# Short four-band TensorE products: the loop over the bands moves inside the loop over terms

## The chip, the core and the metric

The kernel runs on one core of a Trainium2 chip. The metric is the device time of one execution in microseconds (us); the kernel before takes 1805.59 us, the median of three runs (1805.42 to 1806.01). TensorE is called PE here, VectorE DVE, ScalarE ACT, GpSimd POOL and SyncE SP.

## What is computed

Two layers work on 128 context and 256 latent tokens of 1024 features. Each layer is a half-step SwiGLU, a mixing sub-layer and another half-step SwiGLU, each behind a norm that is modulated by a conditioning vector. The modulation is a product of that vector with a matrix of 1024 x 9216 per layer:

```python
mod = (jax.nn.silu(cond) @ P['w_mod'][l] + P['b_mod'][l]).reshape(cond.shape[0], N_MOD, 1, D_MODEL)
...
z = h @ P['w_in'][l]
z_a, z_b, z_c = jnp.split(z, [S5_WIDTH, S5_WIDTH + 2 * CONV_WIDTH], axis=-1)
y_a, h_final = _s5_branch(z_a, P, l, h0)
```

One branch of the mixer is a complex-diagonal state-space scan (S5) with 32 groups of 16 channels and 64 states per direction. The kernel runs the scan in chunks of eight tokens, and for that it computes tables on the chip from the S5 parameters: a matrix from a chunk's inputs to the state, one from the state to the outputs, and the kernel inside a chunk, which is the product of the first factor of one (`bp`, `bb`) with the other (`my`, `cT`, `nci`).

## The kernel before

PE's instructions run in the order in which the program is written; the other engines have an order of their own, laid down when the program is built. Almost all of PE's work is the large projections: each weight unit (512 KB) is fetched by SP's queue into `wr`, split by ACT (`wh`, line 126) and DVE (`wl`, line 105) into a high and a low part, and multiplied in three passes (lines 198 to 200), 24 products of 384 columns for a full unit. Three buffers hold the splits, so a new split can begin only when PE has left the unit three before it. After each unit the projection calls `tick()`, which lets side work go one step on: modulation (`mod_group`, line 385, and `mod_wide`, line 427), the S5 tables (`s5_tables`), and the mixer's own side steps.

`s5_tables(l)` goes through 32 groups, four at a time: eight **blocks** per layer, sixteen in all. In a block DVE first makes `my` and `mt` over several ticks. Then PE writes one PSUM bank in four bands of 32 partitions, one band for each group `s`: two terms `i` of `bp` with `my` over 128 columns (line 1013), then two terms over 16 columns from `bb` with `cT` and `nci` (line 1022). ACT copies the bank to `kall` (line 1030). PE then turns eight 128 x 128 tiles of `mt` (line 138): four into the other bank of the two in `ps_tb`, four into the first bank again, for which they need the copy to `kall` to be over. ACT copies both (`ms`, line 1038). POOL's queue sends `my`, `ms` and `kall` to memory.

`mod_wide` sums weighted rows on DVE into two accumulators and ends with a similar product (line 427): four bands, two terms `i`, 256 columns. It runs four times. `mod_group` (line 385) has four bands too, but there the loop over the bands `s` is already the innermost, inside the loop over `k`.

Both operands of these products are f32, and the profile shows such a product as two records; a line that is run 128 times has 256 records.

Of the kernel before, what the change touches and what calls it, by code (L numbers as in the profile page):

```python
# [16 lines left out]
PSUM = bass.MemoryType.PSUM  # L17
# [18 lines left out]
H = 16  # L36
# [20 lines left out]
def hybrid_step(ctx: ExitStack, tc: tile.TileContext, I, pos_r, pos_c, y_prompt, y_sample, new_state):  # L57
# [70 lines left out]

# [1 line left out]
    ident = cst.tile([P, P], F32, tag="ident", name="ident")  # L130
# [8 lines left out]

# [1 line left out]
    early = {"on": True}  # L141
# [62 lines left out]

    # short products, spread among the long ones
    small = deque()
# [34 lines left out]
    def proj(srcs, xs, nt=NT, kfirst=False, between=None):  # L241
        """PSUM tiles [feature tile, tokens] of xs @ src for each [K, 256] source in turn, alternating along K."""
        n = srcs[0].shape[0] // P
        out = [(mm_bank(), mm_bank()) for _ in srcs]
        for k0, k1 in kparts(n):
            for s, o in zip(srcs, out):
                u = next_unit(s[k0 * P : k1 * P, :])
                if kfirst:
                    order = [(k, m) for k in range(k0, k1) for m in range(2)]
                else:  # L250
                    order = [(k, m) for m in range(2) for k in range(k0, k1)]
                for k, m in order:
                    mm3(o[m][:, :nt], u, xs[k], k - k0, mcols(m), k == 0, k == n - 1)
                    if between and m:
                        between()
                tick()
        return out if len(srcs) > 1 else out[0]

# [1 line left out]
    x = [cst.tile([P, NT], F32, tag=f"x{k}", name=f"x{k}") for k in range(KD)]  # L260
# [30 lines left out]

# [1 line left out]
    pv_t = []  # L293
# [38 lines left out]

# [1 line left out]
    silu_c = cst.tile([P, KD, 32], F32, tag="silu_c", name="silu_c")  # L334
# [18 lines left out]
    def mod_group(l, q):  # L353
        """q: 2048 columns from 2048 q on, or (0, half): that half of the tiles of the first shift and scale"""
        half = isinstance(q, tuple)
# [55 lines left out]
    def mod_wide(l, c0, n=WU):  # L411
        """n columns from c0 on, summed over the 128-row tiles ahead of the tensor engine's sum over the rows"""
        acc = [c4([P, WU], f"macc{s}") for s in range(2)]
        for k in range(KD):
            raw = m6([P, WU], "modw")
            nc.sync.dma_start(raw, I["w_mod"][l][k * P : (k + 1) * P, c0 : c0 + WU])
            for s in range(2):
                if k == 0:
                    act.activation(acc[s], raw, AF.Copy, scale=silu_c[:, k, s : s + 1])
                else:  # L420
                    stt(acc[s], raw, silu_c[:, k, s : s + 1], acc[s])
                yield
        w = WU // 4
        b = ax_bank()
        for s in range(4):
            for i in range(2):
                pe.matmul(
                    b[32 * s : 32 * s + 32, :w],
                    pick[:, i, :],
                    acc[i][:, s * w : (s + 1) * w],  # L430
                    start=(i == 0),
                    stop=(i == 1),
                    skip_group_check=True,
                )
        yield
        mod_out(l, b, [c0 + s * w for s in range(4)], w)
        yield
# [23 lines left out]

# [1 line left out]
    class Stats:  # L463
# [17 lines left out]
        def preload(self, t):  # L481
            """the square root's table, ahead of its use"""
            act.activation(self.std[:, 3:4], t[:, 0:1], AF.Sqrt, bias=eps_t)
            self.loaded = True
# [15 lines left out]
    def bcast_diag(dg):  # L500
        """[128 tokens, 3] on diagonals -> every partition holds all 384 values (in PSUM)."""
        b = ax_bank()
# [3 lines left out]
    class Lead:  # L506
        """The norm in front of a sub-layer.

        The first products take x times the norm's and the modulation's scales, with the shifts as two more
        columns, and the root mean square divides their results; by then the normed tokens are there for the rest.  # L510
        """

# [53 lines left out]
        def result(self, b):  # L566
            """(product over the root mean square, what the shifts add to it) of a first product's bank"""
            t = tmp("ld")
# [6 lines left out]
    class First:  # L575
        """The norm of the tokens as they come in: the modulation arrives last, in halves of the features."""

# [47 lines left out]

# [1 line left out]
    def ffn_srcs(l, j):  # L627
# [71 lines left out]

# [1 line left out]
    ms_d = [drm.tile([P, G, 2, P], F32, tag=f"ms{l}", name=f"ms{l}") for l in range(DEPTH)]  # L701
# [42 lines left out]
    def exp_(out, a, w):  # L744
        """out <- exp(a): 2^k times the series of the remainder; w: four scratch planes"""
        xx, kk, rr, pp = (w[:, i] for i in range(4))
# [29 lines left out]
    def s5_params(raw, ldt):  # L776
# [20 lines left out]
        yield  # L797
        # sine and cosine of a_im dt: reduced to [-pi, pi], then the half angle's series
        mul(th, aim, dtb)
# [32 lines left out]
        br, bi = pw[:, 0, 1], pw[:, 1, 1]  # L832
        # q = (abar - 1) / a
        mul(den, are, are)
# [12 lines left out]
        yield  # L847
        # powers of abar
        done = 1
        while done < TC:  # L850
# [5 lines left out]
            yield  # L856
        # powers as the chunk matrices need them: [to state, from state]
        lo_i = slice(TC - 1, None, -1), slice(1, TC + 1)
# [10 lines left out]
        yield  # L869
        # unit rotation per chunk  # L870
        cur = e1
# [40 lines left out]
    def s5_tables(l):  # L912
# [25 lines left out]
        for gb in range(G // GB):  # L938
# [24 lines left out]
            for sb in range(GB // GS):  # L963
# [44 lines left out]
                b = tb_bank()  # L1008
                for s in range(4):
                    g = s0 + s  # L1010
                    rows = slice(32 * s, 32 * s + 32)
                    for i in range(2):
                        pe.matmul(  # L1013
                            b[rows, : TC * H],
                            bp[:, i, g, :],
                            my[:, s, i].rearrange("p i h -> p (i h)"),
# [3 lines left out]
                        )  # L1020
                    for i in range(2):
                        pe.matmul(  # L1022
                            b[rows, TC * H : 9 * H],
                            bb[:, i, g, :],
                            cT[:, 0, g, :] if i == 0 else nci[:, g, :],
                            start=(i == 0),
# [26 lines left out]

# [1 line left out]
    def gelu_sig(t, src):  # L1055
        """t <- sigmoid of the tanh form's argument, so that gelu(src) = src * t"""
        act.activation(t, src, AF.Square, scale=math.sqrt(GELU_A))
# [30 lines left out]
    def mixer(l, ld, nxt):  # L1088
# [6 lines left out]

        # incoming states of the latent sequence
        srow = s1([P, 2, PS, 2], "srow")[:G]
        gq.dma_start(srow, I["state_ssm"][0, l].rearrange("d g p r -> g d p r"))
        h0 = s1([P, 2, G], "h0")

        # S5 input
        zd = drm.tile([G, H, TC, NCH], F32, tag=f"z_d{l}", name="z_d")
# [158 lines left out]
        def activate(t):  # L1261
# [3 lines left out]
            y2 = tmp("y2")  # L1265
            ci = lambda v: v.rearrange("p (c i) -> p c i", i=TC)  # noqa: E731
            stt(ci(y2), zp[:, t].rearrange("p (j c) -> p c j", j=TC), pv[:, 48 + t : 49 + t], ci(b[:, :NT]))
# [19 lines left out]

        # spatial gating
        sg = {}
# [17 lines left out]
        def sg_bias():  # L1307
            # ln_b[c] * sum_k w[q, k] + b[q], for the folded affine of the norm
            b = tb_bank()
# [82 lines left out]

        # conv branch
        pads = []
# [66 lines left out]
        def side():  # L1461
            f = lambda fn, *a: (fn, a)  # noqa: E731
            tap = [f(conv_taps, j, min(j + 3, CONV_K)) for j in range(0, CONV_K, 3)]
# [47 lines left out]

        # spatial gating: first half, feature major
        bu = ld.proj(cols(w_in, 1024))
        for m in range(2):
# [3 lines left out]
            us.append(t)  # L1518
        # spatial gating: second half, token major
        b3 = [mm_bank(), mm_bank(), ax_bank()]  # L1520
# [15 lines left out]

        # conv input
        bb2 = proj([cols(w_in, 768)], hs)
# [14 lines left out]

        # branches, gated
        def gate(br, n):
# [77 lines left out]

# [1 line left out]
    def mod_all(l, qs, after):  # L1635
# [32 lines left out]
    class Final:  # L1668
        """The last norm: tokens times its scale, turned token major; the root mean square divides at the end."""

# [128 lines left out]
def _positions():  # L1799
    """Separable grid embedding, feature major: row part [128, 4, rows], column part [128, 4, width]."""  # L1800
    import numpy as np
# [39 lines left out]
```

## Time and profile before

| | us |
|---|---|
| median of the runs | 1805.59 |
| profiled execution, from first to last instruction | 1802.9 |
| PE busy | 1778.9 |
| ACT waiting for line 1022 (16 times) | 21.2 |

The runs count 2.7 us that lie around the span. A record of PE has a start and a modelled end; successive products overlap in their tails, so durations must not be added up: the distance from one start to the next is what a record costs. "PE" are products, "PEld" the loads of the stationary operand in front of each.

### The profile page before, as it was taken

To read this page: it belongs to the slowest core of one execution; us is meant where nothing else is said; L and a number is where in the kernel's file an instruction comes from. 1 tells how busy PE (TensorE), PEld (TensorE's weight loads), DVE (VectorE), ACT (ScalarE), POOL (GpSimd) and SP (SyncE) were. 2 spreads that over 40 slices of the span, in tenths; PEclk is the share of its full clock that TensorE was granted. 3 is DMA by queue.
4 is the path that set the end of the run, shared out by engine and by line. 5 is a ranking of instruction groups with operands and counts; after the bars stand their busy time and mean duration, and the time that the engine had idled before them with its cause. 6 is when DMAs were issued, how large, how long until landed. Compare 5 with 4: busy or idle time off the path is not lost.

```text
span 1802.9 us, 29079 instructions
## 1 busy us (share of the span) xinstructions
PE 1778.9 (99%) x11186; PEld 1695.1 (94%) x11186; DVE 1248.1 (69%) x2344; ACT 796.0 (44%) x1330; POOL 202.8 (11%) x400
## 2 busy tenths in 40 slices
PE   7999999999999999999999999999999999999997
PEld 4898999999999989999999899999999999999997
DVE  5495676678996786679386665766799787544445
ACT  4354333475455553233366233245834546423233
POOL 2012343310010000000001133232100000000000
PEclk9999999999999999999999999999999999999999
DMA  9768677666743566778346766557666433434332
GB/s 343 249 217 288 210 237 259 213 197 175 250 144 123 173 229 219 254 271 257 117 129 205 243 203 204 179 187 218 172 198 185 138 124 116 135 123 128 129 123 77
DMA packets 253746, 344.37 MB, mean 191 GB/s; under 512 B 22399, under 2 KB 216651, under 8 KB 253608
## 3 DMA queue, kind: packets, MB, share of 16 engines
q1 hardware_dynamic: 228504, 299.18, 51.7%
q0 software_dynamic: 17088, 39.51, 7.3%
q10 hardware_dynamic: 8016, 3.82, 0.8%
q8 instruction: 88, 1.44, 0.3%
q14 instruction: 50, 0.41, 0.1%
HBM read 309.75 MB, written 32.70 MB: 190 GB/s over the span
## 4 chain that ended last, share of the span: by engine, by line
PE 94%; DVE 2%; DMA 2%; ACT 1%; issue 1%; SPq 0%; DVEq 0%; ACTq 0%
PE mm L198 28%; PE mm L199 28%; PE mm L200 27%; PE ax L385 3%; PE tb L1013 1%; PE tb L1159 1%; PE tb L138 1%; PE tb L1237 1%; DMA modw<-in_w_mod_dram 1%; DMA wr<-in_w_in_dram 1%; DVE wl L105 0%; DVE macc L123 0%; PE ax L503 0%; PE tb L1022 0%; PE ax L138 0%
## 5 line engine op out<-in xcount | busy, mean ns | idle before, releaser
L105 DVE TENSOR_TENSOR wl<-wr,wh 128x1024 fp32r<-128x1024 f32 (+2 forms) x389 | 457.1, 1175 | 367.9 <-ACT wh L126 363.2
L126 ACT ACTIVATE wh<-wr 128x1024 fp32r<-128x1024 f32 (+1 forms) x387 | 395.7, 1023 | 650.2 <-PE mm L199 467.4
L198 PE MATMUL mm<-hh,wh 128*128 128x384 f32 x1840 | 628.1, 341 | 3.1 <-ACT hh L609 3.1
L199 PE MATMUL mm<-hl,wh 128*128 128x384 f32 x1840 | 616.4, 335 | 0.7 <-DVE hl L105 0.7
L200 PE MATMUL mm<-hh,wl 128*128 128x384 f32 x1840 | 616.3, 335 | 0.0
L198 PEld LDWEIGHTS mm<-hh,wh 128*128 128x128 f32 x1840 | 346.0, 188 | 32.6 <-issue 20.1
L199 PEld LDWEIGHTS mm<-hl,wh 128*128 128x128 f32 x1840 | 346.2, 188 | 1.6 <-DVE hl L105 1.2
L200 PEld LDWEIGHTS mm<-hh,wl 128*128 128x128 f32 x1840 | 345.9, 188 | 0.1
L198 PE MATMUL mm<-ah,wh 128*128 128x384 f32 x800 | 271.7, 340 | 0.0
L199 PE MATMUL mm<-al,wh 128*128 128x384 f32 x800 | 269.7, 337 | 0.6 <-DVE al L105 0.6
L200 PE MATMUL mm<-ah,wl 128*128 128x384 f32 x800 | 269.3, 337 | 0.0
L198 PEld LDWEIGHTS mm<-ah,wh 128*128 128x128 f32 x800 | 150.2, 188 | 9.6 <-issue 6.7
L199 PEld LDWEIGHTS mm<-al,wh 128*128 128x128 f32 x800 | 150.2, 188 | 0.9 <-DVE al L105 0.9
L200 PEld LDWEIGHTS mm<-ah,wl 128*128 128x128 f32 x800 | 150.2, 188 | 0.0
L123 DVE SCALAR_TENSOR_TENSOR x<-mm,gt,x 128x128 f32<-128x128 f32 x224 | 83.1, 410 | 33.6 <-PE mm L200 33.1
L198 PE MATMUL mm<-xh,wh 128*128 128x386 f32 x240 | 84.6, 353 | 0.0
L199 PE MATMUL mm<-xl,wh 128*128 128x386 f32 x240 | 82.1, 342 | 0.0
L200 PE MATMUL mm<-xh,wl 128*128 128x386 f32 x240 | 82.0, 342 | 0.0
L126 ACT ACTIVATE ah<-av 128x384 fp32r<-128x384 f32 x82 | 42.1, 518 | 87.0 <-DVE av L105 86.7
L123 DVE SCALAR_TENSOR_TENSOR macc<-modw,silu_c,macc 128x1024 f32<-128x1024 f32 x56 | 69.9, 1277 | 11.0 <-DMA modw<-in_w_mod_dram 10.9
L123 DVE SCALAR_TENSOR_TENSOR cacc<-pad,pv,cacc 128x399 f32<-128x399 f32 x120 | 68.5, 627 | 0.0
L385 PE MATMUL ax<-modw,silu_c 128*32 128x512 f32 (+1 forms) x576 | 63.0, 513 | 0.0
(316 smaller groups left out, 1941.0 us busy)
## 6 DMA issues: line engine op xcount, KB each, us to landing
wr<-in_ffn_w_dram SPq DMA_DIRECT2D x256, 512.0 KB, 3.5
modw<-in_w_mod_dram SPq DMA_DIRECT2D x144, 512.0 KB, 5.0
wr<-in_w_gate_dram SPq DMA_DIRECT2D x48, 512.0 KB, 4.6
wr<-in_w_in_dram SPq DMA_DIRECT2D x24, 512.0 KB, 3.8
my<-my POOLq DMA_DIRECT2D x16, 512.0 KB, 5.1
ms<-ms POOLq DMA_DIRECT2D x16, 512.0 KB, 4.0
m_ms<-ms SPq DMA_DIRECT2D x16, 512.0 KB, 6.7
m_my<-my SPq DMA_DIRECT2D x16, 512.0 KB, 9.9
```

The lines of the kernel that those rows point to most:

```text
L105: (eng or dve).tensor_tensor(out, a, b, op=op)
L123: dve.scalar_tensor_tensor(out, a, s, b, op0=op0, op1=op1)
L126: act.activation(hi, full, AF.Copy)
L138: pe.transpose(out, in_, ident[:rows, :rows])
L198: pe.matmul(out, wh[:, k, cols], xh, start=first, stop=False)
L199: pe.matmul(out, wh[:, k, cols], xl, start=False, stop=False)
L200: pe.matmul(out, wl[:, k, cols], xh, start=False, stop=last)
L385: pe.matmul(b[32 * s : 32 * s + 32, :w], silu_c[:, k, :], raws[i][:, c : c + w], start=(k == 0), stop=(k == KD - 1), skip_group_check=True,)
L1013: pe.matmul(b[rows, : TC * H], bp[:, i, g, :], my[:, s, i].rearrange("p i h -> p (i h)"), start=(i == 0), stop=(i == 1), skip_group_check= ...
L1159: pe.matmul(b[:, g * NCH : (g + 1) * NCH], d["ms"][g // GS][:, g % GS, i, :], U[:, q * GB + g, :], start=True, stop=True,)
L1237: pe.matmul(b[64 * half : 64 * half + NCH, g * P : (g + 1) * P], u, w, start=(n == 0), stop=(n == 2), skip_group_check=True,)
```

## The change

In both places the loop over the bands goes inside the loop over the terms. Before, a band got all its products before the next band got its first; after, each term goes to all four bands before the next term. In the tables the 16-column products, which stood at the end of each band, now stand behind all the 128-column ones. The products, their operands, the bank and the order of the terms inside a band are the same, and nothing is added or removed on any engine. (Comments go too, which moves line numbers.)

```diff
@@ mod_wide
-        for s in range(4):
-            for i in range(2):
+        for i in range(2):
+            for s in range(4):
                 pe.matmul(
                     b[32 * s : 32 * s + 32, :w],
                     pick[:, i, :],
@@ s5_tables
-                for s in range(4):
-                    g = s0 + s
-                    rows = slice(32 * s, 32 * s + 32)
-                    for i in range(2):
+                for i in range(2):
+                    for s in range(4):
                         pe.matmul(
-                            b[rows, : TC * H],
-                            bp[:, i, g, :],
+                            b[32 * s : 32 * s + 32, : TC * H],
+                            bp[:, i, s0 + s, :],
                             my[:, s, i].rearrange("p i h -> p (i h)"),
                             start=(i == 0),
                             stop=(i == 1),
                             skip_group_check=True,
                         )
-                    for i in range(2):
+                for i in range(2):
+                    for s in range(4):
                         pe.matmul(
-                            b[rows, TC * H : 9 * H],
-                            bb[:, i, g, :],
-                            cT[:, 0, g, :] if i == 0 else nci[:, g, :],
+                            b[32 * s : 32 * s + 32, TC * H : 9 * H],
+                            bb[:, i, s0 + s, :],
+                            cT[:, 0, s0 + s, :] if i == 0 else nci[:, s0 + s, :],
                             start=(i == 0),
                             stop=(i == 1),
                             skip_group_check=True,
                         )
```

## Rows read from the trace of the kernel before

**Rows 1.** The page: busy time of the engines; the chain by engine

```profile
PE 1778.9 (99%) x11186; PEld 1695.1 (94%) x11186; DVE 1248.1 (69%) x2344; ACT 796.0 (44%) x1330; POOL 202.8 (11%) x400
...
PE 94%; DVE 2%; DMA 2%; ACT 1%; issue 1%; SPq 0%; DVEq 0%; ACTq 0%
```

**Rows 2.** Windows of the two stretches with blocks: busy us, granted clock, DMA share, GB/s

```profile
170.00:350.00 180.00, 180.00 (x1239) 165.24 (x1239) 122.35 (x207) 65.04 (x107) 61.23 (x116) 1.00 0.73 231
1020.00:1235.00 215.00, 215.00 (x1452) 202.96 (x1451) 138.41 (x235) 75.67 (x118) 63.74 (x120) 1.00 0.61 193
```

**Rows 3.** Waits: engine, tile, line, releaser: us in total, times, longest

```profile
ACT wh L126 <- PE mm L199: 467.4, 221, 5.8
DVE wl L105 <- ACT wh L126: 363.2, 211, 6.0
...
ACT kall L1030 <- PE tb L1022: 21.2, 16, 2.0
...
PEld mm L198 <- ACT wh L126: 7.1, 9, 0.8
```

**Rows 4.** Groups of instructions by line and shape, PE: count, busy us, mean ns

```profile
L1013 PE MATMUL tb<-my,bp 128*32 128x128 f32 x256 | 32.3, 278 | 0.0
...
L427 PE MATMUL ax<-macc,pick 128*32 128x256 f32 x64 | 4.3, 384 | 0.0
```

**Rows 5.** Timeline of PE through one block: start us, us, line, records

```profile
178.68 0.33 PE L199 MATMUL mm<-hl,wh 128*128 128x384 f32 x1
178.86 0.34 PE L200 MATMUL mm<-hh,wl 128*128 128x384 f32 x1
179.12 0.62 PE L1013 MATMUL tb<-my,bp 128*32 128x128 f32 x4
179.59 0.18 PE L1022 MATMUL tb<-cT,bb 128*32 128x16 f32 x1
179.59 0.30 PE L1013 MATMUL tb<-my,bp 128*32 128x128 f32 x1
...
179.65 0.21 PE L1022 MATMUL tb<-nci,bb 128*32 128x16 f32 x2
...
180.53 0.30 PE L1013 MATMUL tb<-my,bp 128*32 128x128 f32 x1
...
180.66 0.49 PE L1013 MATMUL tb<-my,bp 128*32 128x128 f32 x3
180.99 0.21 PE L1022 MATMUL tb<-cT,bb 128*32 128x16 f32 x2
...
181.19 1.11 PE L138 MATMUL tb<-ident,mt 128*128 128x128 f32 x8
182.05 0.42 PE L198 MATMUL mm<-hh,wh 128*128 128x384 f32 x1
```

**Rows 6.** Timeline of PE: a modulation product, bands innermost, 16 records

```profile
19.42 1.07 PE L385 MATMUL ax<-modw,silu_c 128*32 128x256 f32 x16
```

**Rows 7.** Timeline of PE: one end of `mod_wide`, bands outermost, 16 records

```profile
720.67 1.08 PE L427 MATMUL ax<-macc,pick 128*32 128x256 f32 x16
```

**Rows 8.** Timeline of PE, from 720.66 to 720.715 alone: records begun by then

```profile
720.67 0.44 PE L427 MATMUL ax<-macc,pick 128*32 128x256 f32 x4
```

**Rows 9.** Timeline of ACT beside two blocks, the second behind a modulation product

```profile
179.10 1.06 ACT L126 ACTIVATE wh<-wr 128x1024 fp32r<-128x1024 f32 x1 [3.95 <-issue]
181.30 0.29 ACT L1030 ACTIVATE kall<-tb 128x144 f32<-128x144 f32 x1 [1.14 <-PE tb L1022]
...
226.33 1.06 ACT L126 ACTIVATE wh<-wr 128x1024 fp32r<-128x1024 f32 x1 [0.81 <-PE mm L199]
227.29 0.51 ACT L126 ACTIVATE ah<-av 128x384 fp32r<-128x384 f32 x1
229.38 0.29 ACT L1030 ACTIVATE kall<-tb 128x144 f32<-128x144 f32 x1 [1.58 <-PE tb L1022]
```

**Rows 10.** Timeline of DVE ahead of the block of group 5: the last `mt`

```profile
175.95 0.68 DVE L105 TENSOR_TENSOR mt<-tp,tp 128x512 f32<-128x512 f32 x1
```

## The prediction

> **What bounds the kernel now.** I read the page's busy times and its chain of waits first, then windows of the stretches in which the changed lines run, then the waits, and last the records of one block on PE with ACT beside it. The reader is to see that PE has work in 99% of the span and holds 94% of the chain [rows 1], and that in the two stretches with blocks it is busy for all of 180 and all of 215 us, at a granted clock of 1.00 (2.4 GHz), while DVE is at 68 and 64%, ACT at 36 and 35% and the DMA engines at 73 and 61% [rows 2]. The other engines are paced by PE: ACT's splits of the weights wait 467.4 us for PE to leave a buffer, and DVE's wait 363.2 us for ACT's, while PE waits 7.1 us in the whole run for a high part, and no wait for a low part is among the long ones [rows 3]. So a microsecond less of PE's own work in these stretches is a microsecond off the end, as long as the splits keep their lead.
>
> Now one block [rows 5]. The first band's record starts at 179.12, the turning of `mt` at 181.19: 2.07 us for 32 records. Inside a band a 128-column record follows the last after 0.11 us (three take 0.49, of which the last 0.27) and a 16-column one after 0.03 (0.21 less 0.18). The bands stand one behind the other: the second starts at 179.59, the last at 180.53, so a band's turn is 0.94 / 2 = 0.47 us. Only at the seams do two bands run at once: at 179.59 the second band's first record starts in the same hundredth as the first band's fifth, and its last three run beside it, still 0.03 us apart.
>
> That overlap is the key. In a modulation product with the bands innermost, 16 records of 256 columns take 1.07 us in all [rows 6]; at 0.38 us for one [rows 4] this leaves (1.07 - 0.38) / 3 = 0.23 us for each of the three further turns of all four bands. The four bands run at the same time. With the bands outermost `mod_wide` takes 1.08 us for the same 16 records [rows 7], and there four of them have begun within 0.05 us [rows 8]: with four records in a band, PE gets to the other bands by itself. With eight in a band it did not, until three were left [rows 5]. Both places fit a PE that can set aside about three records of a band while it looks for work of another.
>
> **The ends of the modulation sums.** Four blocks of 16 records go from the form of rows 7 to that of rows 6: 4 x 0.01 us, nothing. Were it to lose, the nearest bound is the 0.05 us in which the bands start, so 4 x 0.05 = 0.2 us either way.
>
> **The table products.** There are sixteen blocks (256 records of line 1013, 16 in each) [rows 4], alike but for what stands ahead of them. With all four bands at once a block lasts as long as one band by itself plus the lag between bands. One band, from its first record to the turning of `mt`, is the last band of rows 5: 181.19 - 180.53 = 0.66 us. The lag: four starts within 0.05 us [rows 8], and a row of 16 records with bands innermost is not longer than three turns and one record [rows 6]; I take 0.02. That makes 0.68 us and saves 2.07 - 0.68 = 1.39 us per block, 16 x 1.39 = **22.2 us**. The bound on the worse side: if the 16-column records shared one stream at 0.03 us each, 12 more would stand in line, 0.36 us a block, 5.8 us in all. At the seam of rows 5 they kept their 0.03 us beside another band's record, so I take nothing for it. The better side has no more than the lag, 0.3 us.
>
> **What is late next: ACT.** The copy to `kall` waits for PE in all sixteen blocks now, 21.2 us [rows 3]. With PE done 1.39 us earlier, ACT is not always free. In twelve blocks, those directly behind a weight unit, ACT takes up a split just as the block starts: at 179.10, for 1.06 us, so until 1.04 us into the block [rows 9]. The next operation of ACT may start 0.10 us ahead of a split's recorded end (227.29 against 226.33 + 1.06) [rows 9]. So the copy starts at about 0.94 and ends, 0.29 later, at 1.23 us. The fifth turn needs its bank. Today the copy ends 181.30 + 0.29 - 181.19 = 0.40 us behind the first turn, and the eight turns take 182.05 - 181.19 = 0.86 us [rows 5], their own pace of 0.11 each. So the copy may end until 0.68 + 0.40 = 1.08 without cost, and PE will wait 0.15 us: 12 x 0.15 = **1.8 us** given back. In the other four blocks a modulation product goes ahead; in one of them ACT is done with its splits at 227.29 + 0.51 = 227.80, and the copy, at 229.38 today, would come at 227.99 [rows 9], so nothing is lost. Bounds: 0, if ACT gets free sooner, and if all sixteen paid 0.3 us (a small operation of ACT in between), 4.8.
>
> **Everything else.** No instruction, DMA or semaphore is added. POOL's DMAs of `kall` and `ms` and SP's weight loads keep their order and start earlier with PE. The products' inputs are early: the last `mt` of the first block is done at 176.63, 2.5 us ahead of it [rows 10]; the least of the sixteen. A block that is 1.3 us shorter takes as much from the lead of the next splits; that the splits wait for PE, by 467.4 / 221 = 2.1 us on the average [rows 3], covers it. If that cover were gone in some ticks, each would give back at most its 1.3 us.
>
> **Sum.** 22.2 - 1.8 + 0.0 = 20.4 us off a span of 1802.9: 1782.5. The median stands 2.7 us above the span, so the runs should read 1805.6 - 20.4 = **1785.2 us**.
>
> **A rule that speaks against it.** In rows 6 to 8 all four bands hold the same stationary operand; in the table each group has its own `bp`. The Trainium skill, "TensorE: Matmul & The Clock Gate", Part 3, says that a load of weights overlaps running products only where the row groups differ, and all bands here use all 128 rows. By that rule each load would wait for the products before it, the bands would still follow one another, and the time would stay. The trace does not bear it out: at 179.59 to 179.65 two bands with different operands run together, loads included [rows 5].
>
> **The rivals.**
> 1. *Bands with different operands do not run together beyond the seam.* Then 32 records stay in line, 1805.6, or PE reorders as it does now and the change says nothing. For it: no row shows four different operands at once. Against it: the seam. Chance 0.05.
> 2. *The 16-column part stays in line*: + 5.8 us, and with the copy then ready at 1.15 us the 1.8 us of waiting vanish: 1785.2 + 5.8 - 1.8 = 1789.2. For it: these records are so short that their loads may set the pace. Against it: the 0.03 us kept at the seam. Chance 0.07.
> 3. *Slower: a change of band costs what entering the four-band form costs.* The first record of a block comes 179.12 - 178.86 = 0.26 us after the last projection product, where the one before it came after 0.18: 0.08 us more [rows 5]. A block now changes band 4 times, after it 16. If each change cost that and kept bands apart, 12 x 0.08 = 0.96 us a block, and 4 x 0.08 in each of four sums: 1805.6 + 15.4 + 1.3 = 1822.3. It decides only if changes both cost over 1.39 / 12 = 0.12 us or forbid the overlap. Against it: rows 6, where the band changes at every product and the time is that of rows 7. Chance 0.03.
>
> **How the numbers follow.** The forecast has a chance of 0.85; its own range is 22.5 to 17.4 us off (copy's wait 0 to 4.8), 1783.1 to 1788.2. To hold eight in ten I reach to rival 2 and leave 1.6 us below for waits elsewhere that may fall otherwise: 1781.5 to 1790. A measurement of this kernel can tell about 0.2% (3.6 us) from no change. Faster by more: 0.85 + 0.07 = 0.92; within: 0.05; slower: 0.03.
>
> **What would show it.** In the profile after, a block's line 1013 records should form four quick groups of four, some 0.11 us apart, and the turning of `mt` begin 0.7 us behind the first; at 0.93 rival 2 holds, at 2.07 rival 1. Twelve copies to `kall` should start close behind a split of ACT and no longer wait for line 1022, whose wait falls from 21.2 to about 3 us. The turns should take 0.95 to 1.0 us in these twelve blocks and 0.86 in four. Line 427 should keep its 1.08 us. The prediction is wrong if PE is no longer busy throughout the two stretches, that is, if a split or a DMA comes too late.

## The result: some 20 us less, nearly all of it in sixteen blocks

| | before | after |
|---|---|---|
| median of the runs, us | 1805.8 (four runs, 1805.42 to 1808.8) | 1784.95 (1782.06 to 1785.44) |
| time over time before, 95% interval | 1 | 0.9877 (0.9864 to 0.989) |
| span of the profiled execution, us | 1802.9 | 1783.6 |
| PE busy, us | 1778.9 | 1758.1 |

The kernel is faster, by 1.2%; the forecast was 1785.2. The first block after, on PE (start us, us, engine, line, records), beside [rows 5]:

```profile
181.08 0.34 PE L200 MATMUL mm<-hh,wl 128*128 128x384 f32 x1
181.35 0.65 PE L1012 MATMUL tb<-my,bp 128*32 128x128 f32 x16
181.81 0.23 PE L1022 MATMUL tb<-cT,bb 128*32 128x16 f32 x8
181.87 0.23 PE L1022 MATMUL tb<-nci,bb 128*32 128x16 f32 x8
182.03 1.24 PE L138 MATMUL tb<-ident,mt 128*128 128x128 f32 x8
183.03 0.42 PE L198 MATMUL mm<-hh,wh 128*128 128x384 f32 x1
```

The reader is to see that line 1012 (line 1013 before) is now one row of 16 records, which last 0.65 us together with a tail of 0.27, that the eight and eight short records follow in steps of 0.03 us, each step with all four bands, and that the turning of `mt` begins 182.03 - 181.35 = 0.68 us after the first record, where it took 2.07. The view cut to the first 0.06 us of the block shows four records begun, the last of them 0.02 us behind the first (0.32 less 0.30):

```profile
181.35 0.32 PE L1012 MATMUL tb<-my,bp 128*32 128x128 f32 x4
```

The stretches with blocks are still all PE (busy us of PE, PEld, DVE, ACT, POOL, then granted clock, DMA share, GB/s), as in [rows 2]:

```profile
170.00:350.00 180.00, 180.00 (x1299) 164.59 (x1298) 129.75 (x223) 69.49 (x115) 66.59 (x126) 1.00 0.78 247
1010.00:1220.00 210.00, 210.00 (x1482) 197.11 (x1481) 141.76 (x244) 77.49 (x123) 67.66 (x127) 1.00 0.66 204
```

PE has 1299 records in the 180 us that held 1239, at the same granted clock, and the DMA engines go from 73 to 78% in the first stretch: the work is packed tighter and nothing else has become the bound. The waits that answer to [rows 3]:

```profile
ACT wh L126 <- PE mm L199: 483.9, 227, 5.8
DVE wl L105 <- ACT wh L126: 350.2, 202, 4.8
...
PEld mm L198 <- ACT wh L126: 7.1, 9, 0.8
```

```profile
ACT kall L1030 <- PE tb L1022: 2.0, 4, 0.7
```

PE waits as little for a split as before, and ACT's wait for line 1022 has fallen from 21.2 us in sixteen places to 2.0 in four.

**Where the time went.** From the first record of a block to the product behind its turns (a projection's, in two blocks a modulation's) PE spends, summed over the sixteen blocks and read from the starts of their rows, 47.1 us before and 26.6 after: 20.5 less. The span loses only 19.3, because this profiled execution happened to get to its first projection product 2.05 us later than the one before (25.47 against 23.42 us from the start). Past that point the two traces keep step unit by unit, but for the sixteen blocks and 0.8 us at one stall behind 824 us that is gone. Elsewhere the time outside the blocks did not change.

### The profile page after: what moved, and what is told of

The parts are those of the page before. It is cut to its first block, busy times and chain, and to the rows that moved or that the text cites. A ratio compares the mean times of both kernels' runs of the same rounds, so it can differ in the third digit from the quotient of the medians.

```text
span 1783.6 us, 29079 instructions
## 1 busy us (share of the span) xinstructions
PE 1758.1 (99%) x11186; PEld 1672.6 (94%) x11186; DVE 1247.1 (70%) x2344; ACT 795.0 (45%) x1330; POOL 202.8 (11%) x400
## 4 chain that ended last, share of the span: by engine, by line
PE 97%; DVE 1%; DMA 1%; ACT 1%; issue 0%; DVEq 0%; ACTq 0%
PE mm L198 30%; PE mm L199 29%; PE mm L200 29%; PE ax L385 3%; PE tb L1159 1%; PE tb L138 1%; PE tb L1237 1%; DMA wr<-in_w_in_dram 1%; PE tb L1012 0%; PE ax L503 0%; PE ax L138 0%; DMA crow<-in_c_dram 0%; DVE sqacc L105 0%; PE mm L1528 0%; PE ax L489 0%; PE mm L1530 0%
## 5 line engine op out<-in xcount | busy, mean ns | idle before, releaser
L123 DVE SCALAR_TENSOR_TENSOR macc<-modw,silu_c,macc 128x1024 f32<-128x1024 f32 x56 | 69.9, 1279 | 10.3 <-DMA modw<-in_w_mod_dram 10.3
```

The source lines that it names most:

```text
L123: dve.scalar_tensor_tensor(out, a, s, b, op0=op0, op1=op1)
```

## The experiments

Every program here has the kernel before beside it on the same chip; its median there was 1807.0 (first four), 1808.3 (next two) and 1805.7 us (last two), so the ratios are what is to be compared, and "us less" below is the ratio times 1805.6.

| | first record to first turn, us | us less, by the blocks' rows | us less, by the ratio (95%) |
|---|---|---|---|
| changed kernel | 0.685 | 20.5 | 22.2 (19.9 to 24.6) |
| tables only | 0.685 | 20.5 | 19.7 (16.8 to 22.6) |
| sums only | 2.07 | 0 | -1.1 (-2.7 to 0.7) |
| bands outermost, runs of 4 and 4 | 0.722 | 20.1 | 19.7 (16.6 to 22.8) |
| bands outermost, runs of 6 and 2 | 1.41 | 10.3 | 10.3 (7.6 to 13.0) |
| bands outermost, run of 8, short ones first | 1.14 | 14.8 | 16.8 (13.9 to 19.7) |

In every row what the blocks save on PE (second column of numbers) lies inside the interval of what the kernel saves (last column): what a block gives up on PE, the kernel gets back.

### Each part alone

The first run keeps the new order in the tables and the old one in `mod_wide`:

```diff
 # mod_wide, against the changed kernel
-        for i in range(2):
-            for s in range(4):
+        for s in range(4):
+            for i in range(2):
```

> Only the table products have the loop over bands innermost; the ends of the modulation sums (line 427) are as before. If the gain is PE time of the sixteen table blocks and nothing else: the block lasts 0.685 us to the first turn of mt as in the changed kernel, and the time is that of the changed kernel, 1785.0, 1.5 either way. If the sums carry a part of it: above 1787.

Measured: 0.9891 (0.9875 to 0.9907) of the kernel before, a median of 1786.46 beside 1807.0, and 0.685 us to the first turn. The interval overlaps that of the changed kernel, and the blocks' rows are the same to 0.01 us. The second run is the opposite, the new order in `mod_wide` alone:

> Only the four ends of the modulation sums have the loop over bands innermost; the tables are as before. If PE gets to all four bands of four records by itself, nothing is to be had: line 427 keeps 1.06 to 1.08 us for its 16 records, table blocks 2.07 us, and the time is 1805.6, 1 either way. If changing bands at every product has a price of its own of 0.08 us (the slower rival): 1.4 us more.

Measured: 1.0006 (0.9996 to 1.0015). One end of the sums on PE:

```profile
723.34 1.05 PE L427 MATMUL ax<-macc,pick 128*32 128x256 f32 x16
724.32 0.44 PE L198 MATMUL mm<-ah,wh 128*128 128x384 f32 x1
```

The 16 records take 1.05 us in place of 1.08 [rows 7], and the product behind them starts 0.98 us after the first of them, 0.03 us sooner. Four times that is 0.1 us: this half of the change does nothing that the time can show, and the slower rival's price for a change of band, 0.08 us, is not paid either.

### Is it the order, or the length of a band's run?

The third run does not put the bands inside. It only takes the 16-column records out of the bands' runs:

```diff
 # s5_tables, against the changed kernel (mod_wide as before, here and in the next two)
-                for i in range(2):
-                    for s in range(4):
+                for s in range(4):
+                    for i in range(2):
...
-                for i in range(2):
-                    for s in range(4):
+                for s in range(4):
+                    for i in range(2):
```

> Bands stay outermost everywhere, as before the change; but the 16-column products of the tables get a loop of their own behind the 128-column ones, so a band has two runs of four records in place of one run of eight. If PE can set aside about three records of a busy band and look past them, four in a run are enough: all four bands start within 0.05 us, the block lasts 0.69 to 0.72 us, and the time is 1785. If it is the change of band at every product that lets bands run together: the bands follow one another, 2.07 us, 1805.6.

```profile
180.45 0.34 PE L1012 MATMUL tb<-my,bp 128*32 128x128 f32 x4
```

```profile
180.45 0.67 PE L1012 MATMUL tb<-my,bp 128*32 128x128 f32 x16
180.91 0.24 PE L1022 MATMUL tb<-cT,bb 128*32 128x16 f32 x6
180.97 0.18 PE L1022 MATMUL tb<-nci,bb 128*32 128x16 f32 x1
...
181.17 1.20 PE L138 MATMUL tb<-ident,mt 128*128 128x128 f32 x8
182.13 0.42 PE L198 MATMUL mm<-hh,wh 128*128 128x384 f32 x1
```

The first row is the view cut to the first 0.05 us: four records have begun, one in each band, while three of each earlier band's four wait. All 16 long records go through in 0.67 us with the bands outermost; the first turn comes after 0.72 us, 0.04 later than in the changed kernel. In six of the twelve blocks behind a weight unit even that is not seen at the end, because the turns wait for the copy anyhow: 1.68 us from the first record to the next projection product (180.45 to 182.13 here), as in the changed kernel (181.35 to 183.03). In the other ten of the sixteen the end comes 0.01 to 0.05 us later. So it is not the change of band at every product that lets the bands run together. The next run makes a band's run six records long:

```diff
 # s5_tables, against the kernel before, shortened
                 for s in range(4):
                     for i in range(2):
                         pe.matmul(b[...], bp[:, i, ...], my[:, s, i]...)
-                    for i in range(2):
+                    for i in range(1):
+                        pe.matmul(b[...], bb[:, i, ...], cT[...])
+                for s in range(4):
+                    for i in range(1, 2):
                         pe.matmul(b[...], bb[:, i, ...], cT[...] if i == 0 else nci[...])
```

> Bands outermost, a run of six records (four of 128 columns, two of 16) in each band, then a run of two for the rest. If PE looks past three records set aside, a band is left when its third record starts, 0.24 us after its first: block 3 x 0.25 + 0.66 = 1.41 us, and no wait for the copy to kall, so 16 x 0.66 = 10.6 us off the kernel before, 1795. If only runs of four and less can overlap: 2.07 us a block, 1805.6. If the length of a run did not matter: 0.69 us, 1785.

```profile
179.21 0.66 PE L1011 MATMUL tb<-my,bp 128*32 128x128 f32 x6
179.67 0.21 PE L1018 MATMUL tb<-cT,bb 128*32 128x16 f32 x2
179.70 0.41 PE L1011 MATMUL tb<-my,bp 128*32 128x128 f32 x4
179.92 0.21 PE L1018 MATMUL tb<-cT,bb 128*32 128x16 f32 x2
...
180.62 1.11 PE L138 MATMUL tb<-ident,mt 128*128 128x128 f32 x8
```

The first turn comes 180.62 - 179.21 = 1.41 us after the first record, to the hundredth what the reading of three records set aside gives. The short pairs of successive bands are 0.25 us apart (179.67, 179.92): the time of the first two long records, after which a band of six has its third record begun and three left. The fifth run goes back to runs of eight and only turns their order round, the short records first:

```diff
 # s5_tables, against the kernel before, shortened
                 for s in range(4):
+                    for i in range(2):
+                        pe.matmul(... bb with cT, nci ...)
                     for i in range(2):
                         pe.matmul(... bp with my ...)
-                    for i in range(2):
-                        pe.matmul(... bb with cT, nci ...)
```

> Bands outermost with a run of eight records as before the change, but the four 16-column records of a band stand ahead of its four 128-column ones. If PE looks past three records set aside, the band is left when its fifth record starts, which is now 0.15 us after its first (four short ones) in place of 0.47: block 3 x 0.15 + 0.66 = 1.11 us, 16 x 0.96 = 15.4 us off the kernel before, 1790. If the number of records in a run is what counts, as such: 2.07 us a block and 1805.6.

```profile
180.04 0.24 PE L1012 MATMUL tb<-cT,bb 128*32 128x16 f32 x2
180.13 0.21 PE L1012 MATMUL tb<-nci,bb 128*32 128x16 f32 x2
180.19 0.28 PE L1021 MATMUL tb<-my,bp 128*32 128x128 f32 x1
180.20 0.24 PE L1012 MATMUL tb<-cT,bb 128*32 128x16 f32 x2
...
180.34 0.28 PE L1021 MATMUL tb<-my,bp 128*32 128x128 f32 x1
180.35 0.23 PE L1012 MATMUL tb<-cT,bb 128*32 128x16 f32 x2
...
181.19 1.11 PE L138 MATMUL tb<-ident,mt 128*128 128x128 f32 x8
```

The second band's first record starts at 180.20, right behind the first band's fifth (180.19), the third's at 180.35, behind the second's fifth (180.34). The first turn comes after 1.14 us (1.11 were expected), and the kernel is 16.8 us faster. With the same eight records in a band, the block falls from 2.07 to 1.14 us, because the fifth record of a band now starts after 0.15 us, not 0.47. Four programs, in which a band reaches its last three records after nothing, 0.15, 0.24 and 0.47 us, give blocks of 0.72, 1.14, 1.41 and 2.07 us. What holds the other bands up is the stretch of a band's run ahead of its last three records. One thing these runs leave open: a product here is always two records, so three waiting records are always the second half of a product that has begun and one product behind it. Whether PE counts records or products, they cannot tell.

### What is late next: the copy to `kall`

After the change the turns of `mt` take longer: in the first block 183.03 - 182.03 = 1.00 us between rows, where it was 0.86 [rows 5]. ACT beside the block after:

```profile
181.32 1.06 ACT L126 ACTIVATE wh<-wr 128x1024 fp32r<-128x1024 f32 x1 [3.95 <-issue]
182.29 0.27 ACT L1030 ACTIVATE kall<-tb 128x144 f32<-128x144 f32 x1
182.72 1.18 ACT L1038 ACTIVATE ms<-tb 128x512 f32<-128x512 f32 x2 [0.16 <-PE tb L138]
```

As foretold the copy starts close behind the split, without waiting for PE: 0.94 us into the block in six of the twelve blocks behind a weight unit, and 0.89 to 0.90 in the other six, where ACT took up its split 0.05 us earlier. The copy's end sets the end of the turns: wherever a projection product follows, before and after, it starts 0.46 to 0.47 us behind the copy's end. It ended 0.40 us behind the first turn before (0.86 to the next product), and ends 0.53 behind it here (1.00). To see what that costs, one run gives the copy to DVE:

```diff
-                act.activation(kall[:, sb, :], b[:, : 9 * H], AF.Copy)
+                dve.tensor_copy(kall[:, sb, :], b[:, : 9 * H])
```

> The changed kernel, with the copy to kall on DVE in place of ACT, where it need not stand behind a split of 1.06 us. If the fifth turn of mt waits for that copy behind ACT's split: from the first turn to the fifth it takes 0.44 to 0.50 us in place of 0.51 to 0.58, and the span loses 1.0 to 1.8 us against the changed kernel, 1783.2 to 1784. If the turns are late for another reason: no change in them. If DVE's copy stands behind a split of DVE instead: up to 1 us more in each such block.

```profile
179.59 0.64 PE L1012 MATMUL tb<-my,bp 128*32 128x128 f32 x16
...
180.44 0.31 DVE L1030 COPY kall<-tb 128x144 f32<-128x144 f32 x1 [2.00 <-PE tb L1022]
180.66 1.22 DVE L105 TENSOR_TENSOR wl<-wr,wh 128x1024 fp32r<-128x1024 f32 x1
```

```profile
200.15 0.62 PE L1012 MATMUL tb<-my,bp 128*32 128x128 f32 x16
...
200.29 1.23 DVE L105 TENSOR_TENSOR wl<-wr,wh 128x1024 fp32r<-128x1024 f32 x1 [2.88 <-ACT wh L126]
...
201.43 0.30 DVE L1030 COPY kall<-tb 128x144 f32<-128x144 f32 x1
```

Measured: 0.9881 (0.9863 to 0.99), no different from the changed kernel in time: the 1.0 to 1.8 us that were expected did not come, and the rows say why. In eleven of the twelve blocks the copy now waits for PE alone, and starts 0.85 to 0.87 us into the block (180.44 here); with ACT it was 0.89 to 0.94. The turns get back only 0.23 us in all twelve together. But DVE's copy is also longer, 0.31 us beside 0.27, which hides up to 0.4 us in twelve blocks. In the four blocks behind a modulation product the copy stands behind a split of DVE (201.43, of a block that starts at 200.15), and these lose 0.5 us each, 2.0 in all. So taking ACT's split away buys little, because another limit lies close behind it: PE gives the bank free later than the prediction had it. The copy started 0.22 us behind the start of the last short record before; it starts 0.27 to 0.30 behind it after the change wherever it waits for PE alone. In the run of six and two, where one band ends alone again, it was 0.22 to 0.25. Why the release is later when four bands end together was not tried.

A last pair of runs takes the cause away: the products of a block are issued two steps of the side work ahead of its turns, and the changed kernel runs beside it.

```diff
-                for _ in range(3):
-                    yield
+                yield
                 b = tb_bank()
 ...
                 act.activation(kall[:, sb, :], b[:, : 9 * H], AF.Copy)
+                yield
+                yield
                 ms = c4([P, GS, 2, P], "ms")
```

> The changed kernel, but the products of a block are issued two steps of the side work ahead of the turns of mt, so a weight unit or more lies between them and the copy to kall has microseconds to spare. If the turns are late in the changed kernel because their second half waits for that copy: from the first turn to the next projection product 0.84 us in all sixteen, in place of 0.89 to 0.97, 1.6 us in all. Leaving the projection twice per block in place of once may cost up to 0.09 us each, 1.4 us. So the time is that of the changed kernel beside it, 0 to 1.6 us less. If the turns are late by themselves: still 0.92 to 0.97 us and 0 to 1.4 us more.

> The changed kernel beside the one before, to be compared on one chip with the run in which products and turns are apart: 0.988 of the kernel before, 20 to 21 us less, and blocks of 0.685 us to the first turn as in its first profile.

```profile
195.10 0.64 PE L1010 MATMUL tb<-my,bp 128*32 128x128 f32 x16
195.56 0.23 PE L1020 MATMUL tb<-cT,bb 128*32 128x16 f32 x8
195.62 0.23 PE L1020 MATMUL tb<-nci,bb 128*32 128x16 f32 x8
195.78 0.45 PE L198 MATMUL mm<-hh,wh 128*128 128x384 f32 x1
```

```profile
180.24 0.34 PE L200 MATMUL mm<-hh,wl 128*128 128x384 f32 x1
180.41 1.03 PE L138 MATMUL tb<-ident,mt 128*128 128x128 f32 x8
181.20 0.42 PE L198 MATMUL mm<-hh,wh 128*128 128x384 f32 x1
```

With the copy out of the way the turns take 181.20 - 180.41 = 0.79 us, and start 0.17 us behind the last projection product, so they pay nothing for standing alone. The waiting for the copy is thereby shown, 0.15 to 0.2 us in each of the twelve blocks behind a weight unit; even the 0.86 us of the kernel before held 0.07 of it. By the rows all sixteen blocks together take 1.6 us less than in the changed kernel beside it, although the four whose turns now follow a modulation product take 0.14 us or more longer, one of them 1.0 (its turns wait 0.8 us for the copy after all). The time is 0.9878 (0.9862 to 0.9895) beside 0.9892 (0.9876 to 0.9907) for the changed kernel on the same chip: the two cannot be told apart by it.

## Why the prediction was right

- **What bounds the kernel.** PE without a gap in both stretches, before and after; the splits kept their lead, and 20.5 us less of PE's work came out as 20 to 22 us less of time. Right. That the median lies 0.25 us from the forecast is in part luck, since the four runs spread over 3.4 us; the 20.5 us of the rows beside the 20.4 of the sum is the better test.
- **The ends of the sums.** Nothing, as forecast: 0.1 us by the rows, 1.0006 by the runs.
- **The table products.** 0.68 us to the first turn was forecast and 0.685 measured in every block behind a weight unit; 16 x 1.38 = 22.1 us, where 22.2 stood in the sum. One band by itself plus a lag of 0.02 us was the right model. Rival 1 asked for 2.07 us. Rival 2 asked for 0.68 + 0.36 = 1.04 by its own price (the 0.93 that was named as its sign does not follow from that price). Neither is there. Four bands with four different stationary operands do run together, so the rule of the Trainium skill ("TensorE: Matmul & The Clock Gate", Part 3), by which loads overlap running products only across row groups, does not describe these column bands: 32 loads and 32 products fit into 0.68 us. [Rows 5] has products alone and could not carry the prediction's "loads included"; these are the loads of the first block after the change:

```profile
181.34 0.38 PEld L1012 LDWEIGHTS tb<-my,bp 128*32 128x32 f32 x16 [0.25 <-issue]
181.70 0.24 PEld L1022 LDWEIGHTS tb<-cT,bb 128*32 128x32 f32 x8
181.84 0.17 PEld L1022 LDWEIGHTS tb<-nci,bb 128*32 128x32 f32 x8
```

- **What is late next.** 1.8 us were to be given back; by the rows of the sixteen blocks the turns take 1.55 us more in all. The place was right and the size nearly, with two steps off that partly cancel. In the twelve blocks behind a weight unit the copy was to end 1.23 us into the block, behind ACT's split, and cost 0.15 us; it ends at 1.21 and costs 0.13 in six, at 1.17 and costs 0.08 in the others, 1.29 us in all. The four blocks behind a modulation product were to lose nothing; they lose 0.05 to 0.08 us each, because there the copy starts 0.27 to 0.30 us behind PE's last record, not 0.22. One reading of the kernel before was wrong: its 0.86 us were taken for the turns' own pace. Without a wait they take 0.79, so the kernel before waited for the copy in every block already, and anything that made the copy later had to cost its full lateness.
- **The slower rival.** Its price for a change of band did not appear in either place: the sums with a change at every product are 0.02 to 0.04 us faster each.
- **What PE looks past.** "About three records of a band" was a reading from two places; four programs with the bands outermost now bear it out, 1.41 us forecast and 1.41 measured, 1.11 and 1.14. That it counts, and does not measure time, is shown by the runs of eight in two orders; whether records or products is open. Over all bands together it can set aside at least nine records (three of each of three bands, in the run of four and four); the most was not tried.

## What to carry to other kernels

When several narrow bands of PE are fed in turn, look at the starts of their records: if the second band starts only when the first is nearly through, the order of issue is the limit, not the array, and interleaving the bands, or just keeping each band's run at four records, packs them four deep. Where a run is already that short, as in the modulation sums, reordering brings nothing. And what stands behind the packed block, here the copy that frees its bank, then has less to hide behind: ask for it before counting the whole gain.

## What was not expected of the hardware

PE took records of a later band ahead of three waiting records of an earlier one wherever the bands stood outermost: in the kernel before the second band's first record starts at 179.59, ahead of the first band's last ones at 179.65 [rows 5]. So the order of the program, which the description of the kernel gives as the order in which PE runs, is not the order of the starts. Taking it that a band is left when three records of its run wait, the blocks with runs of 4, 6 and 8 come out within 0.03 us of what was expected (0.72, 1.41 and 1.14 us). A block of 32 records left its bank to the copy 0.27 to 0.30 us behind the start of its last record when four bands ended together, and 0.22 us when one band ended alone in the kernel before (0.22 to 0.25 in the run of six and two).
